# Differential attention: map 1's exponentials in PSUM, the scale in the queries, low query halves on 128 rows, shorter column steps

## Chip, cores and metric

The kernel runs on one core of one Trainium2 chip. The metric is device time in microseconds (us) of one execution, the median over several runs; lower is better. A profiled execution gives, beside its time, a trace with every engine's instructions: TensorE (PE, with its weight loads as PEld), VectorE (DVE), ScalarE (ACT), GpSimd (POOL) and SyncE's DMA queue (SPq).

## Reference

A two-layer diffusion backbone: 512 latent tokens, 256 context tokens, width 1024, one batch, fp32. Layer 0 mixes tokens with DeltaNet and retention heads, layer 1 with differential attention, and each layer ends in a convolutional feed-forward block. The change lies nearly all in layer 1's attention, 8 heads, each with two softmax maps of head size 64 over 768 keys and values of 128 columns:

```
def diff_mix(q, k, v, lam):
    """q (2,B,H,Lq,d), k (2,B,H,Lk,d), v (B,H,Lk,dv): (softmax(q1 k1) - lam softmax(q2 k2)) v."""
    s = jnp.einsum('cbhqd,cbhkd->cbhqk', q, k).astype(jnp.float32) * DIFF_HD ** -0.5
    p = jax.nn.softmax(s, -1)
    a = p[0] - lam * p[1]
    return jnp.einsum('bhqk,bhkd->bhqd', a.astype(v.dtype), v)
...
    def finish(o):
        o = rms_norm(o) * subln_w.astype(f32) * (1.0 - lambda_init)
        return (merge_heads(o).astype(w_out.dtype) @ w_out).astype(h.dtype)
```

Before it, `project` forms q, k and v from the layer's input and turns q and k by rotary angles. Only the 512 latent tokens are queries here.

## The kernel before

A scheduler places every instruction: the program is a sequence of tile operations with priorities, and each engine then has a fixed order that follows from them. Instructions wait on semaphores for their operands and for buffers to come free.

The attention is done head pair by head pair, four pairs. While `attend` works on pair p, the projections of pair p+1 (`project`) fill TensorE between its steps; during the last pair the filler is the output projection (`sums`). A matrix product of fp32 quality is made of three products of rounded halves ("hi" and "lo", names whi, wlo, hTh, hTl): every projection tile is a chain of `opj` matmuls of 128x256, three for each block of the inner dimension. DVE and POOL make the low halves of the weights (line 148), ACT the high ones (line 147).

`project` ends, for queries, with a rotation (`rope`: DVE lines 1575 and 1579, POOL line 1581), four transposes into a PSUM tile `oT_ps`, and `q_evac`, which takes that tile apart into SBUF tiles `oq`. The low 64 partitions (LO) hold map 0, the high 64 (HI) map 1. Tile q[0] holds map 0's rounded queries, in both halves of the partitions; q[1] does so for map 1; q[2] has the remainders, map 0 in LO and map 1 in HI. Keys (`ok`, `k_evac`) carry the rounded value in one half of the partitions and the remainder in the other, so one matmul over 128 rows gives q_hi*(k_hi + k_lo). `oT_ps` and `opj` share two PSUM buffers ("wo").

A step of `attend` is one of a head's four query tiles: 8 steps in a pair, 32 in all. A step does

- scores: for each map, two matmuls over 128 rows (512 and 256 columns) into a PSUM tile `sc` (two buffers for all), then two over the 64 rows of q[2],
- for each map: a row maximum `mx` on DVE (line 1665), its scaling on DVE (1666), the exponential on ACT (1668) into the SBUF tile `pt`, row sums into `Zs` (in the trace oZ),
- the factor `nl` on DVE (1672, 1673), one column, and the combination pt0 + nl*pt1 on DVE (1676), 768 columns,
- six transposes of pt into `aT_ps`, copies to `aT` by ACT (four blocks) and DVE (two, line 1684), six matmuls with the values into the same `aT_ps`, a copy to `oall` on DVE (1688) and a square on ACT (1689) for the norm.

After a head's four steps the norm is closed by a chain of 128x4 operations on DVE: lines 1693 to 1695, an rsqrt by iteration (lines 127 to 136, names rs_h, rs_y, rs_w), line 1697, and four products of 128x128 (1699).

Of the kernel before, what the change touches and what calls it, by code (L numbers as in the profile page):

```python
# [20 lines left out]
P = 128  # L21
# [76 lines left out]
class Net:  # L98
# [177 lines left out]
    def setup(self):  # L276
# [22 lines left out]
        self.cpad = cp.tile([P, KT, 32], F32, name="cpad")  # L299
        nc.gpsimd.memset(self.cpad, 0.0)  # L300
# [218 lines left out]
    def even_mixer(self, accst):  # L519
        w_in = self.a["e_w_in"][0]  # L520
        with ExitStack() as outer:
            with ExitStack() as right:
                p2 = self.pool(right, "d2", bufs=2, side="right")
                self.p2b = lambda: self.pool(right, "d2b", bufs=2, side="right")
# [1015 lines left out]
    def odd_mixer(self, acc_st):  # L1540
        nc, a = self.nc, self.a
        v, g, s_ = nc.vector, nc.gpsimd, nc.scalar
        with ExitStack() as st0:
            y = self.hT
            pj = self.pool(st0, "ps_opj", bufs=2, space=PSUM)
            with ExitStack() as st:
# [13 lines left out]
                lp = cpl.tile([P, 4, DH], F32, name="lp")  # L1560
                nc.scalar.dma_start(out=lp, in_=a["o_lambda"][0].partition_broadcast(P))
                l2 = cpl.tile([P, 2], F32, name="l2")
                for i in range(2):
                    v.tensor_mul(lp[:, 2 * i], lp[:, 2 * i], lp[:, 2 * i + 1])
                    v.reduce_sum(l2[:, i:i + 1], lp[:, 2 * i], axis=AX.X)
                s_.activation(l2, l2, AF.Exp)
                nlam = cpl.tile([P, 1], F32, name="nlam")
                v.tensor_sub(nlam, l2[:, 1:2], l2[:, 0:1])
                v.tensor_scalar_add(nlam, nlam, -LAMBDA_INIT)

                def rope(ps, t, out):

                    pv, ov = (x.rearrange("p (t h f n) -> p t h f n", t=2, h=4, f=2) for x in (ps, out))
                    b = p2.tile([P, 2, 4, 2, 32], F32, tag="ob", name="ob")
# [26 lines left out]
                def project(pr, passes, hd):  # L1601
# [3 lines left out]
                    hd["q"] = [hp.tile([P, 2, LAT], F32R, tag=f"oq{j}", name="oq") for j in range(3)]  # L1605
# [40 lines left out]
                def attend(h, q, k, vt, i):  # L1646
# [4 lines left out]
                    for t in range(NLT):  # L1651
                        pr = []
                        scs = [scp.tile([P, 1024], F32, tag="sc", name="sc") for c in range(2)]
                        for c in range(2):
                            for k0, n in ((0, 512), (512, 256)):
                                self.mm(scs[c][:, k0:k0 + n], q[c][:, i, t * P:(t + 1) * P], k[c][:, i, k0:k0 + n],
                                        stop=False)

                        for k0, n in ((0, 512), (512, 256)):
                            for c, rows in enumerate((LO, HI)):  # L1660
                                self.mm(scs[c][:, k0:k0 + n], q[2][rows, i, t * P:(t + 1) * P], k[c][rows, i, k0:k0 + n],
                                        start=False)
                        for c, sc in enumerate(scs):
                            mx = pb.tile([P, 1], F32, tag="mx", name="mx")
# [5 lines left out]
                            pr.append(pt)  # L1670
# [144 lines left out]
```

## Time and profile before

| | us |
|---|---|
| median of three runs (lowest, highest) | 2107.94 (2104.75, 2113.5) |
| the profiled execution | 2102.7 |
| its span in the trace | 2100.9 |
| PE busy | 1961.3 (93%) |
| DVE, POOL, ACT busy | 1272.7, 777.8, 703.8 |

The trace's time axis begins with the span. The attention of layer 1 lies between 1326 and 1665 us: the first three pairs up to 1592, the last pair behind it. The projections of its first pair lie ahead of it, from about 1255. PE's rows give a start and a duration; a matmul's end is modelled and overlaps the next one's start, so what one costs is read from start to start. A bracket behind a row gives the idle time ahead of it on its engine and what released it.

### The profile page before, as it was taken

To read this page: it belongs to the slowest core of one execution; us is meant where nothing else is said; L and a number is where in the kernel's file an instruction comes from. 1 tells how busy PE (TensorE), PEld (TensorE's weight loads), DVE (VectorE), ACT (ScalarE), POOL (GpSimd) and SP (SyncE) were. 2 spreads that over 40 slices of the span, in tenths; PEclk is the share of its full clock that TensorE was granted. 3 is DMA by queue.
4 is the path that set the end of the run, shared out by engine and by line. 5 is a ranking of instruction groups with operands and counts; after the bars stand their busy time and mean duration, and the time that the engine had idled before them with its cause. 6 is when DMAs were issued, how large, how long until landed. Compare 5 with 4: busy or idle time off the path is not lost. (4 is left out here: it accounts for less than half of the span.)

```text
span 2100.9 us, 33593 instructions
## 1 busy us (share of the span) xinstructions
PE 1961.3 (93%) x13766; PEld 1668.8 (79%) x13766; DVE 1272.7 (61%) x2534; ACT 703.8 (33%) x1228; POOL 777.8 (37%) x412
## 2 busy tenths in 40 slices
PE   6989999999898999999999998999897989999997
PEld 4777677878898988888888877878786887888886
DVE  2354755544358676565656574567667688756567
ACT  3331343423244422222222243444444443323231
POOL 1233223212322344444444433212123036666572
PEclk8999999999999999999999999999997999999999
DMA  8546344455523321111111112011102223232221
GB/s 264 161 129 177 110 133 139 146 172 173 171 81 121 115 76 61 61 61 61 61 61 61 61 61 68 21 41 41 41 31 71 80 101 121 94 106 96 85 81 40
DMA packets 195586, 201.34 MB, mean 96 GB/s; under 512 B 21112, under 2 KB 183512, under 8 KB 195432
## 3 DMA queue, kind: packets, MB, share of 16 engines
q1 hardware_dynamic: 194136, 197.57, 29.9%
q8 instruction: 108, 1.77, 0.4%
q10 hardware_dynamic: 1296, 1.62, 0.3%
q14 instruction: 46, 0.38, 0.1%
HBM read 185.89 MB, written 13.27 MB: 95 GB/s over the span
## 5 line engine op out<-in xcount | busy, mean ns | idle before, releaser
L148 POOL TENSOR_TENSOR wlo<-raw,whi 128x2048 fp32r<-128x2048 f32 (+2 forms) x154 | 413.2, 2709 | 490.1 <-ACT whi L147 457.1
L1442 DVE SCALAR_TENSOR_TENSOR ac<-g_ps,fconvT,ac 128x441 f32<-128x441 f32 (+2 forms) x352 | 243.6, 694 | 190.7 <-ACT ac L1431 181.0
L147 ACT CAST whi<-raw 128x2048 fp32r<-128x2048 f32 (+2 forms) x177 | 200.4, 1169 | 373.7 <-PE d_ps L115 162.2
L115 PE MATMUL d_ps<-whi,hh 128*128 128x512 f32 x440 | 176.1, 400 | 11.5 <-DVE gt L1391 6.6
L115 PE MATMUL d_ps<-wlo,hh 128*128 128x512 f32 x440 | 172.9, 393 | 0.0
L115 PE MATMUL d_ps<-whi,hl 128*128 128x512 f32 x440 | 172.3, 392 | 0.6 <-DVE hl L148 0.6
L115 PE MATMUL opj<-whi,hTh 128*128 128x256 f32 x512 | 151.3, 295 | 1.1 <-ACT oq L1592 1.1
L115 PE MATMUL g_ps<-hTl,whi 128*128 128x512 f32 (+1 forms) x384 | 145.1, 378 | 2.9 <-POOL hTl L148 2.9
L115 PE MATMUL opj<-whi,hTl 128*128 128x256 f32 x512 | 147.4, 288 | 0.0
L115 PE MATMUL opj<-wlo,hTh 128*128 128x256 f32 x512 | 147.2, 288 | 0.0
L115 PE MATMUL u_ps<-hTh,whi 128*128 128x512 f32 (+1 forms) x384 | 144.7, 377 | 0.0
L115 PE MATMUL u_ps<-hTh,wlo 128*128 128x512 f32 (+1 forms) x384 | 144.6, 377 | 0.0
L115 PE MATMUL u_ps<-hTl,whi 128*128 128x512 f32 (+1 forms) x384 | 144.6, 376 | 0.0
L115 PE MATMUL g_ps<-hTh,whi 128*128 128x512 f32 (+1 forms) x384 | 144.5, 376 | 0.0
L115 PE MATMUL g_ps<-hTh,wlo 128*128 128x512 f32 (+1 forms) x384 | 144.2, 376 | 0.0
L115 PE MATMUL fpj<-whi,hTh 128*128 128x256 f32 x432 | 127.0, 294 | 5.6 <-DVE kT L550 4.7
L115 PE MATMUL fpj<-wlo,hTh 128*128 128x256 f32 x432 | 127.0, 294 | 0.0
L115 PE MATMUL fpj<-whi,hTl 128*128 128x256 f32 x432 | 126.0, 292 | 0.0
L115 PEld LDWEIGHTS d_ps<-whi,hh 128*128 128x128 f32 x440 | 82.9, 188 | 38.9 <-DVE gt L1391 17.0
L115 PEld LDWEIGHTS opj<-whi,hTh 128*128 128x128 f32 x512 | 98.4, 192 | 7.2 <-issue 4.5
L115 PEld LDWEIGHTS opj<-whi,hTl 128*128 128x128 f32 x512 | 98.3, 192 | 2.8 <-issue 2.4
L115 PEld LDWEIGHTS opj<-wlo,hTh 128*128 128x128 f32 x512 | 98.5, 192 | 2.3 <-issue 1.2
(465 smaller groups left out, 5023.0 us busy)
## 6 DMA issues: line engine op xcount, KB each, us to landing
mraw<-in_mod_w_dram SPq DMA_DIRECT2D x80, 512.0 KB
raw<-in_f_w_gate_dram SPq DMA_DIRECT2D x22, 1024.0 KB
raw<-in_f_w_up_dram SPq DMA_DIRECT2D x22, 1024.0 KB
raw<-in_f_w_down_dram SPq DMA_DIRECT2D x22, 1024.0 KB
raw<-in_o_w_qkv_dram SPq DMA_DIRECT2D x12, 1024.0 KB
raw<-in_e_w_in_dram SPq DMA_DIRECT2D x10, 1024.0 KB
mraw<-in_mod_w_dram SPq DMA_DIRECT2D x32, 256.0 KB
raw<-in_e_w_in_dram SPq DMA_DIRECT2D x12, 512.0 KB
```

Of the source, the lines that this page charges most:

```text
L115: self.nc.tensor.matmul(out, lhsT=lhsT, rhs=rhs, start=start, stop=stop)
L147: self.nc.scalar.copy(h, r)
L148: lo_eng.tensor_sub(l, r, h.bitcast(F32))
L1442: v.scalar_tensor_tensor(out=o, in0=pv[:, r0 + di:r1 + di, c0 + dj:c1 + dj], scalar=cw[(di + 1) * 3 + dj + 1], in1=o, op0=ALU.mult, op1=AL ...
```

## The change

1. Scores. There are four query tiles: q[0] and q[1] as before, and q[2], q[3] hold the remainders of map 0 and map 1, each in both halves of the partitions. A step's low matmuls go over 128 rows, two for each map, and stand directly behind that map's high ones.
2. The factor 64^-0.5 is multiplied into the queries in `q_evac`. An evacuation has six ACT operations where it had four, and its two DVE operations become scalar_tensor_tensor. The maximum comes out negated from the reduction; the 64 scalings of mx are gone, and so is the scale of the exponential.
3. Map 1's exponential is written over its own scores in PSUM; the combination reads it there. The `sc` buffer of map 1 is read for the last time by the combination (before: by the exponential).
4. `nl` is made by a tensor_scalar with two column operands in place of a scalar_tensor_tensor.
5. The end of a head loses a reciprocal and three 128x4 products on DVE, and gains a 128x4 square on ACT and a 128x4 addition on DVE.
6. Buffers: `cpad`, a constant, moves into a pool of layer 0's mixer; the small tiles for lambda are in a pool of their own that is closed at once; `ob` has one buffer in place of two.

```
 def q_evac(q, ps, cs):
-    s_.copy(q[0][LO, :, cs], ps[LO])
-    s_.copy(q[1][HI, :, cs], ps[HI])
-    v.tensor_sub(q[2][LO, :, cs], ps[LO], q[0][LO, :, cs].bitcast(F32))
-    v.tensor_sub(q[2][HI, :, cs], ps[HI], q[1][HI, :, cs].bitcast(F32))
-    s_.copy(q[0][HI, :, cs], ps[LO])
-    s_.copy(q[1][LO, :, cs], ps[HI])
+    for c, src in enumerate((ps[LO], ps[HI])):
+        own, other = (LO, HI) if c == 0 else (HI, LO)
+        s_.activation(q[c][own, :, cs], src, AF.Copy, scale=DH ** -0.5)
+        v.scalar_tensor_tensor(out=q[2 + c][own, :, cs], in0=src, scalar=DH ** -0.5,
+                               in1=q[c][own, :, cs].bitcast(F32), op0=ALU.mult, op1=ALU.subtract)
+        s_.activation(q[c][other, :, cs], src, AF.Copy, scale=DH ** -0.5)
+        s_.copy(q[2 + c][other, :, cs], q[2 + c][own, :, cs].bitcast(F32))
...
 for c in range(2):
-    for k0, n in ((0, 512), (512, 256)):
-        self.mm(scs[c][:, k0:k0 + n], q[c][:, i, t * P:(t + 1) * P], k[c][:, i, k0:k0 + n],
-                stop=False)
-for k0, n in ((0, 512), (512, 256)):
-    for c, rows in enumerate((LO, HI)):
-        self.mm(scs[c][:, k0:k0 + n], q[2][rows, i, t * P:(t + 1) * P], k[c][rows, i, k0:k0 + n],
-                start=False)
+    for j in (0, 2):
+        for k0, n in ((0, 512), (512, 256)):
+            self.mm(scs[c][:, k0:k0 + n], q[j + c][:, i, t * P:(t + 1) * P],
+                    k[c][:, i, k0:k0 + n], start=(j == 0), stop=(j == 2))
 for c, sc in enumerate(scs):
     mx = pb.tile([P, 1], F32, tag="mx", name="mx")
-    v.reduce_max(mx, sc[:, :TOK], axis=AX.X)
-    v.tensor_scalar_mul(mx, mx, -(DH ** -0.5))
-    pt = pb.tile([P, TOK], F32, tag=f"p{c}", bufs=2 - c, name="pt")
-    s_.activation(pt, sc[:, :TOK], AF.Exp, scale=DH ** -0.5, bias=mx[:, 0:1],
-                  accum_out=Zs[:, t, c:c + 1])
+    v.reduce_max(mx, sc[:, :TOK], axis=AX.X, negate=True)
+    p = pb.tile([P, TOK], F32, tag="p0", name="pt") if c == 0 else sc[:, :TOK]
+    s_.activation(p, sc[:, :TOK], AF.Exp, bias=mx[:, 0:1], accum_out=Zs[:, t, c:c + 1])
...
-v.scalar_tensor_tensor(out=nl, in0=nl, scalar=Zs[:, t, 0:1], in1=nlam,
-                       op0=ALU.mult, op1=ALU.mult)
-v.scalar_tensor_tensor(out=pr[0], in0=pr[1], scalar=nl[:, 0:1], in1=pr[0],
+v.tensor_scalar(out=nl, in0=nl, scalar1=Zs[:, t, 0:1], scalar2=nlam[:, 0:1],
+                op0=ALU.mult, op1=ALU.mult)
+v.scalar_tensor_tensor(out=pt, in0=scs[1][:, :TOK], scalar=nl[:, 0:1], in1=pt,
                        op0=ALU.mult, op1=ALU.add)
...
-rz = pb.tile([P, NLT], F32, tag="orz", name="orz")
-v.reciprocal(rz, Zs[:, :, 0])
-v.tensor_mul(ss, ss, rz)
-v.tensor_mul(ss, ss, rz)
-r = self.rsqrt(pb, ss, NLT, 1.0 / (2 * DH), NORM_EPS, "on")
-v.tensor_mul(r, r, rz)
+zz = pb.tile([P, NLT], F32, tag="orz", name="orz")
+s_.activation(zz, Zs[:, :, 0], AF.Square, scale=math.sqrt(2 * DH * NORM_EPS))
+v.tensor_add(ss, ss, zz)
+r = self.rsqrt(pb, ss, NLT, 1.0 / (2 * DH), 0.0, "on")
```

The instructions' order on three engines, each at one place. First PE in a step of the first pair that alternates with projections, row by row (in the trace 1403.4 to 1407.8 us). Rows give line, operation, tiles and output; `sc` of 128x512 and 128x256 are score matmuls. The first row of before is the step's last high piece, the four `sc` rows behind it are its low ones:

```order
6955 L115 MATMUL sc<-ok,oq 128x256
6956 L115 MATMUL opj<-whi,hTh 128x256
6957 L115 MATMUL sc<-ok,oq 128x512
6958 L115 MATMUL opj<-wlo,hTh 128x256
6959 L119 MATMUL aT_ps<-ident,pt 128x128 x6
6960 L115 MATMUL sc<-ok,oq 128x512
6961 L115 MATMUL opj<-whi,hTl 128x256
6962 L115 MATMUL sc<-ok,oq 128x256
6963 L115 MATMUL opj<-whi,hTh 128x256
6964 L115 MATMUL sc<-ok,oq 128x256
6965 L115 MATMUL aT_ps<-ov,aT 128x128 x6
```

And after, from that step's second map on:

```order
6964 L115 MATMUL sc<-ok,oq 128x512
6965 L115 MATMUL opj<-whi,hTh 128x256
6966 L115 MATMUL sc<-ok,oq 128x256
6967 L115 MATMUL aT_ps<-ov,aT 128x128 x6
6968 L115 MATMUL opj<-wlo,hTh 128x256
6969 L115 MATMUL sc<-ok,oq 128x512
6970 L115 MATMUL opj<-whi,hTl 128x256
6971 L115 MATMUL sc<-ok,oq 128x256
6972 L115 MATMUL opj<-whi,hTh 128x256
```

Score and projection matmuls still alternate; the low matmuls moved from the end of the step into each map's own group of four.

Second, ACT at the first evacuation of queries that falls into the first pair's steps (at 1372.8 us in the trace; they are the second pair's queries); the numbers behind names tell tiles apart (`oT_ps_13311` and `oT_ps_13312` are the same tile of before and after). Before:

```order
612 L1587 CAST oq_12939<-oT_ps_13311 64x2x256
613 L1588 CAST oq_12940<-oT_ps_13311 64x2x256
614 L1591 CAST oq_12939<-oT_ps_13311 64x2x256
615 L1592 CAST oq_12940<-oT_ps_13311 64x2x256
616 L147 CAST whi_13835<-raw_13833 128x2048
617 L1668 ACTIVATE pt_13500,oZ_13486<-sc_13487,mx_13497 128x768
618 L1668 ACTIVATE pt_13505,oZ_13486<-sc_13488,mx_13502 128x768
```

And after:

```order
618 L1591 ACTIVATE oq_12945<-oT_ps_13312 64x2x256
619 L1594 ACTIVATE oq_12945<-oT_ps_13312 64x2x256
620 L1595 CAST oq_12947<-oq_12947 64x2x256
621 L1591 ACTIVATE oq_12946<-oT_ps_13312 64x2x256
622 L1666 ACTIVATE pt_13499,oZ_13486<-sc_13487,mx_13497 128x768
623 L1666 ACTIVATE sc_13488,oZ_13486<-sc_13488,mx_13501 128x768
624 L1594 ACTIVATE oq_12946<-oT_ps_13312 64x2x256
625 L1595 CAST oq_12948<-oq_12948 64x2x256
626 L147 CAST whi_13819<-raw_13817 128x2048
```

The last read of `oT_ps`, row 615 before and row 624 now, moved behind both exponentials of a step.

Third, DVE at the end of the first pair's second head, with the combination of the step that runs beside it (L1676 before, L1674 now). Before:

```order
1445 L1672 RECIPROCAL nl<-oZ 128x1
1446 L134 TENSOR_TENSOR rs_w<-rs_y 128x4
1447 L1673 SCALAR_TENSOR_TENSOR nl<-nl,oZ,nlam 128x1
1448 L135 TENSOR_TENSOR rs_w<-rs_w,rs_h 128x4
1449 L1688 COPY oall<-aT_ps 128x128
1450 L136 SCALAR_TENSOR_TENSOR rs_y<-rs_w,rs_y 128x4
1451 L1676 SCALAR_TENSOR_TENSOR pt<-pt,nl 128x768
1452 L1697 TENSOR_TENSOR rs_y<-rs_y,orz 128x4
1453 L1699 SCALAR_TENSOR_TENSOR oall<-oall,rs_y,sub 128x128 x4
```

And after:

```order
1432 L135 TENSOR_TENSOR rs_w<-rs_w,rs_h 128x4
1433 L1670 RECIPROCAL nl<-oZ 128x1
1434 L1686 COPY oall<-aT_ps 128x128
1435 L136 SCALAR_TENSOR_TENSOR rs_y<-rs_w,rs_y 128x4
1436 L1671 TENSOR_SCALAR nl<-nl,oZ,nlam 128x1
1437 L1696 SCALAR_TENSOR_TENSOR oall<-oall,rs_y,sub 128x128 x4
1438 L1674 SCALAR_TENSOR_TENSOR pt<-sc,nl,pt 128x768
```

The combination moved from ahead of the four products of the head's end to behind them.

## Rows read from the trace of the kernel before

**Rows 1.** The page, section 1: busy us, share of the span, instructions.

```profile
PE 1961.3 (93%) x13766; PEld 1668.8 (79%) x13766; DVE 1272.7 (61%) x2534; ACT 703.8 (33%) x1228; POOL 777.8 (37%) x412
```

**Rows 2.** Windows: length, busy PE PEld DVE ACT POOL (instructions), PEclk, DMA share, GB/s.

```profile
1326.00:1592.00 266.00, 245.61 (x1797) 217.63 (x1796) 169.66 (x371) 113.20 (x224) 54.75 (x21) 0.99 0.11 37
1592.00:1665.00 73.00, 61.76 (x372) 50.08 (x371) 58.53 (x127) 34.99 (x75) 19.71 (x5) 0.84 0.20 66
```

**Rows 3.** PE's waits, first three pairs: us in total, times, longest us.

```profile
PE aT_ps L119 <- DVE pt L1676: 14.3, 10, 3.0
PE oT_ps L119 <- POOL otok L1581: 4.6, 6, 2.4
PE opj L115 <- ACT oq L1592: 1.1, 3, 0.6
```

**Rows 4.** PE's waits, 1255 to 1326 us, where layer 1's projections start.

```profile
PE ln_ps L119 <- ACT acc L1240: 4.1, 2, 2.8
```

**Rows 5.** Timeline of PE: a step whose maps go together (start, us, line, operation).

```profile
1372.49 1.49 PE L115 MATMUL sc<-ok,oq 128*128 128x512 f32 x8
1373.91 0.39 PE L115 MATMUL opj<-whi,hTh 128*128 128x256 f32 x1
```

**Rows 6.** Timeline of PE: one map of a step that goes map by map.

```profile
1326.32 1.05 PE L115 MATMUL sc<-ok,oq 128*128 128x512 f32 x4
1327.30 0.39 PE L115 MATMUL opj<-whi,hTh 128*128 128x256 f32 x1
```

**Rows 7.** Timeline of PE: a step that alternates with projection matmuls.

```profile
1403.43 0.40 PE L115 MATMUL sc<-ok,oq 128*128 128x512 f32 x1
1403.67 0.28 PE L115 MATMUL opj<-whi,hTh 128*128 128x256 f32 x1
1403.79 0.28 PE L115 MATMUL sc<-ok,oq 128*128 128x256 f32 x1
...
1405.36 0.81 PE L119 MATMUL aT_ps<-ident,pt 128*128 128x128 f32 x6
1406.10 0.50 PE L115 MATMUL sc<-ok,oq 64*128 64x512 f32 x1
...
1407.79 0.38 PE L115 MATMUL aT_ps<-ov,aT 128*128 128x128 f32 x1
```

**Rows 8.** Timeline of all engines around one factor nl.

```profile
1380.76 4.54 POOL L148 TENSOR_TENSOR wlo<-raw,whi 128x2048 fp32r<-128x2048 f32 x1
...
1381.15 4.17 DVE L1673 SCALAR_TENSOR_TENSOR nl<-nl,oZ,nlam 128x1 f32<-128x1 f32 x1
```

**Rows 9.** Tile nl, whole span: duration ns min/median/max, first and last start.

```profile
L1673 DVE SCALAR_TENSOR_TENSOR nl<-nl,oZ,nlam x32: 208/219/4168, 1334.6 to 1659.4; 128x1 f32<-128x1 f32 x32
L1676 DVE SCALAR_TENSOR_TENSOR pt<-pt,nl x32: 1006/1018/1020, 1334.8 to 1659.6; 128x768 f32<-128x768 f32 x32
```

**Rows 10.** Tile mx, whole span.

```profile
L1666 DVE TENSOR_SCALAR mx<-mx x64: 127/144/156, 1329.8 to 1657.3; 128x1 f32<-128x1 f32 x64
L1668 ACT ACTIVATE pt<-sc,mx x64: 881/902/914, 1330.0 to 1657.5; 128x768 f32<-128x768 f32 x64
```

**Rows 11.** Timeline of DVE in the last pair.

```profile
1610.62 0.14 DVE L1666 TENSOR_SCALAR mx<-mx 128x1 f32<-128x1 f32 x1
...
1611.55 3.63 DVE L1697 TENSOR_TENSOR rs_y<-rs_y,orz 128x4 f32<-128x4 f32 x1
```

**Rows 12.** Timeline of POOL in the same stretch.

```profile
1605.76 9.40 POOL L185 TENSOR_TENSOR raw<-raw,gate 128x2048 f32<-128x2048 f32 x2 [12.48 <-DMA raw<-in_o_w_out_dram]
```

**Rows 13.** Timeline of ACT and DVE: one evacuation of a query tile.

```profile
1373.56 1.14 DVE L1699 SCALAR_TENSOR_TENSOR oall<-oall,rs_y,sub 128x128 f32<-128x128 f32 x4
...
1374.62 0.68 DVE L1589 TENSOR_TENSOR oq<-oT_ps,oq 64x512 fp32r<-64x512 f32 x1
...
1376.03 0.58 ACT L1591 CAST oq<-oT_ps 64x512 fp32r<-64x512 f32 x1 [2.09 <-DVE oq L1590]
```

**Rows 14.** Tile ac (feed-forward): a DVE operation with one PSUM and one SBUF input.

```profile
L1442 DVE SCALAR_TENSOR_TENSOR ac<-g_ps,fconvT,ac x352: 662/678/745, 700.8 to 2067.1; 128x441 f32<-128x441 f32 x88, 128x504 f32<-128x504 f32 x44, 128x448 f32<-128x448 f32 x44
```

More of the change, by code (lines that the diff above doesn't have):

```diff
@@ L298, in setup @@
         nc.vector.memset(self.lneps, LN_EPS)
-        self.cpad = cp.tile([P, KT, 32], F32, name="cpad")
-        nc.gpsimd.memset(self.cpad, 0.0)
         self.hs = {}
@@ L523, in even_mixer @@
                 p2 = self.pool(right, "d2", bufs=2, side="right")
+                self.cpad = p2.tile([P, KT, 32], F32, bufs=1, name="cpad")
+                self.nc.gpsimd.memset(self.cpad, 0.0)
                 self.p2b = lambda: self.pool(right, "d2b", bufs=2, side="right")
@@ L1559, in odd_mixer @@
                 v.tensor_scalar_mul(sub, sub, 1.0 - LAMBDA_INIT)
[L1560 to L1566, printed above, removed]
-                nlam = cpl.tile([P, 1], F32, name="nlam")
-                v.tensor_sub(nlam, l2[:, 1:2], l2[:, 0:1])
-                v.tensor_scalar_add(nlam, nlam, -LAMBDA_INIT)
+                nlam = cpl.tile([P, 1], F32, name="nlam")
+                with ExitStack() as tmp:
+                    lpp = self.pool(tmp, "olp")
+                    lp = lpp.tile([P, 4, DH], F32, name="lp")
+                    nc.scalar.dma_start(out=lp, in_=a["o_lambda"][0].partition_broadcast(P))
+                    l2 = lpp.tile([P, 2], F32, name="l2")
+                    for i in range(2):
+                        v.tensor_mul(lp[:, 2 * i], lp[:, 2 * i], lp[:, 2 * i + 1])
+                        v.reduce_sum(l2[:, i:i + 1], lp[:, 2 * i], axis=AX.X)
+                    s_.activation(l2, l2, AF.Exp)
+                    v.tensor_sub(nlam, l2[:, 1:2], l2[:, 0:1])
+                    v.tensor_scalar_add(nlam, nlam, -LAMBDA_INIT)
                 def rope(ps, t, out):
                     pv, ov = (x.rearrange("p (t h f n) -> p t h f n", t=2, h=4, f=2) for x in (ps, out))
-                    b = p2.tile([P, 2, 4, 2, 32], F32, tag="ob", name="ob")
+                    b = p2.tile([P, 2, 4, 2, 32], F32, tag="ob", bufs=1, name="ob")
                     v.tensor_mul(out.rearrange("p (t x n) -> p t x n", t=2, n=32),
@@ L1604, in project @@
                     hp = odd if pr % 2 else even
-                    hd["q"] = [hp.tile([P, 2, LAT], F32R, tag=f"oq{j}", name="oq") for j in range(3)]
+                    hd["q"] = [hp.tile([P, 2, LAT], F32R, tag=f"oq{j}", name="oq") for j in range(4)]
                     hd["k"] = [hp.tile([P, 2, TOK], F32R, tag=f"ok{j}", name="ok") for j in range(2)]
@@ L1670, in attend @@
-                            pr.append(pt)
+                            v.reduce_max(mx, sc[:, :TOK], axis=AX.X, negate=True)
+                            p = pb.tile([P, TOK], F32, tag="p0", name="pt") if c == 0 else sc[:, :TOK]
+                            s_.activation(p, sc[:, :TOK], AF.Exp, bias=mx[:, 0:1], accum_out=Zs[:, t, c:c + 1])
+                            if c == 0:
+                                pt = p
                         nl = pb.tile([P, 1], F32, tag="nl", name="nl")
                         v.reciprocal(nl, Zs[:, t, 1:2])
-                        v.scalar_tensor_tensor(out=nl, in0=nl, scalar=Zs[:, t, 0:1], in1=nlam,
-                                               op0=ALU.mult, op1=ALU.mult)
@@ L1681, in attend @@
                             for j in range(n):
-                                self.tr(ps[:, j * P:(j + 1) * P], pr[0][:, (c0 + j) * P:(c0 + j + 1) * P])
+                                self.tr(ps[:, j * P:(j + 1) * P], pt[:, (c0 + j) * P:(c0 + j + 1) * P])
                             eng = s_.copy if n == 4 else v.tensor_copy
@@ L1688, in attend @@
                         v.tensor_copy(oall[:, t, hc], o)
-                        s_.activation(pr[0][:, :P], oall[:, t, hc], AF.Square, accum_out=ss[:, t:t + 1])
+                        s_.activation(pt[:, :P], oall[:, t, hc], AF.Square, accum_out=ss[:, t:t + 1])
                         if t < NLT - 1:
                             yield
-                    rz = pb.tile([P, NLT], F32, tag="orz", name="orz")
-                    v.reciprocal(rz, Zs[:, :, 0])
-                    v.tensor_mul(ss, ss, rz)
-                    v.tensor_mul(ss, ss, rz)
-                    r = self.rsqrt(pb, ss, NLT, 1.0 / (2 * DH), NORM_EPS, "on")
-                    v.tensor_mul(r, r, rz)
+                    zz = pb.tile([P, NLT], F32, tag="orz", name="orz")
+                    s_.activation(zz, Zs[:, :, 0], AF.Square, scale=math.sqrt(2 * DH * NORM_EPS))
+                    v.tensor_add(ss, ss, zz)
+                    r = self.rsqrt(pb, ss, NLT, 1.0 / (2 * DH), 0.0, "on")
                     for t in range(NLT):
```

1 line of the change is left out of this document (removed).

## The prediction, made before the changed kernel ran

> **What bounds the kernel now.** I read the page's busy shares first: PE is busy 93% of the span [rows 1], so time is gained where PE does less or waits less. Then the windows over layer 1's attention, the only long stretch that the change touches [rows 2]. In the first three pairs PE is busy 245.6 of 266 us: PE sets the pace, and its 20.4 us of idle time are waits. In the last pair, 73 us, PE has 11.2 us without work, the granted clock is 0.84 of full speed, and DVE is busy 58.5: there the chain of DVE and ACT operations of each step counts, and PE's matmuls do not. PE's waits in the first three pairs [rows 3] are in the main for the combination, 14.3 us in ten waits, then 4.6 us for POOL's part of the rotation, which the change leaves alone.
>
> Why the combination is late is seen on all engines' timeline [rows 8]: a POOL operation of 4.54 us starts, the factor nl, one column, begins 0.39 us later on DVE and takes 4.17 us, up to the end of POOL's. Undisturbed it takes 0.22 us (the median over 32), the longest 4.17 [rows 9].
>
> **Scores on 128 rows.** Read from start to start, a full-row matmul of 512 columns takes 0.24 us and one of 256 takes 0.12 [rows 7]. After the change a step has four of each: 1.44 us. Before, a step's cost depends on its neighbours. Where both maps go together, the eight matmuls counted by the row and their low pairs take 1373.91 - 1372.49 = 1.42 us [rows 5]: nothing to gain. Where maps go one at a time, a map takes 1327.30 - 1326.32 = 0.98 us, 1.96 a step [rows 6]: 0.52 to gain. Where the pieces alternate with projections, the step spans 1407.79 - 1403.43 = 4.36 us, of which seven projection matmuls of 0.12 (0.84) and six transposes (1406.10 - 1405.36 = 0.74) are not its own; 2.78 remain [rows 7]: 1.34 to gain. By the order on PE each of the three pairs has four steps of the first kind; the first pair has two each of the others (3.7 us), the next two have three of the dearest and one of the middle kind (4.5 us each). Sum 12.7 us; I take **-13**. Bounds: all twelve at 0.52, 6; all at 1.34, 16. The last pair is not paced by PE: nothing.
>
> The Trainium skill speaks against this edit (TensorEngine Tiling (Array Packing), Key Properties): different tiles can execute in parallel, so two 64-row matmuls could cost one, and a change of mode drains the array. By the first half alone the paired steps would lose 0.36 us each by going to 128 rows, 4 us over the twelve of the first three pairs. The row of the paired step shows no such parallel gain (1.42 us, the same as full rows); its second half agrees with what the alternating step pays.
>
> **nl as a tensor_scalar, map 1 in PSUM.** Is a 128x1 tensor_scalar still held up by POOL? The 64 scalings of mx are that form, with one column operand fewer, and none took over 0.156 us [rows 10]. One of them, at 1610.62, took 0.14 while POOL worked and a two-input operation begun 0.93 us later took 3.63 [rows 11, 12]. So I take 0.2 us always. The combination then has one PSUM and one SBUF input; of that form 352 operations of 441 to 504 columns took 0.66 to 0.75 us and never more [rows 14], some 1.0 to 1.1 for 768 columns by proportion, as now (1.02, [rows 9]). The stall goes. The exponential written to PSUM: no row has ACT writing there; I take the 0.90 us of now [rows 10]. Below it a gain of at most the same 0.9 is conceivable, above it twice the time; in the first three pairs either is hidden, since ACT is busy 113 of 266 us, in the last pair twice the time would cost up to 8 x 0.9 = 7 us.
>
> The Trainium skill would have it otherwise (SBUF — State Buffer, Who interferes with whom): tensor_scalar can enter a two-port mode and then contends with GpSimd, whoever comes first blocking the other. By it the new nl would be held as the old one was; the rows of the one-column scalings are against that, so I give it a small chance, as the fourth rival.
>
> **What is late next.** With the stall gone, PE waits for other things. (a) The first evacuation of queries in each pair. Now ACT's last two reads begin at 1376.03 and end at 1377.2 [rows 13]; PE's next projection tile needs that PSUM buffer and waits 0.6 us at most [rows 3]. In the order after, the fourth read of oT_ps stands behind the third copy and two exponentials: DVE's part still starts at 1374.62 (a head's four products are ahead of it), then 0.68, three ACT operations of 0.58, two exponentials of 0.9 and 0.58: 1374.62 + 0.68 + 1.74 + 1.8 + 0.58 = 1379.4, so 2.2 us later. (b) The second evacuation has the same form, with an exponential fewer in front of PE's need: 1.3 us, where the longest wait for a combination (3.0) was. (c) At the end of a pair the combination now stands behind the head's rsqrt chain and its four products on DVE. The products take 1.14 us [rows 13], the chain's share is not to be had from one row; with transposes and copies that come late in turn I take 3.5 us, between 1.1 and twice the longest wait of now, 6. (d) 0.5 for what is left. In all 7.5 us a pair, 22.5 for three, against 20.4 now: **+2**. Bounds: if these waits fall into PE's remaining projection work, only the 4.6 + 1.1 us of the rotation and the old q wait stay, -15; if each is half as long again, +13.
>
> **Removed work on DVE**: 64 scalings at 0.144 (9.2 us) and four small operations a head. In the first three pairs DVE is busy 170 of 266 us, so it is hidden behind PE. 16 more ACT copies of 0.58 us (9.3) are hidden too, but for the place in (a), (b).
>
> **Last pair.** Each of eight steps has a chain shorter by two scalings and their hand-overs (0.3 us), and the first exponential starts a maximum earlier, but three POOL operations still hold the rsqrt chain, whose column products have two SBUF inputs [rows 11, 12]: 8 x 0.3 = 2.4, less what is waited for anyway. I take **-2**, bounds -6 (one stall as in [rows 8] gone as well) and +5 (a step later by the new place of the combination).
>
> **Start of layer 1 and layer 0.** PE's transposes of the new input come 12 projection matmuls later in the order, 12 x 0.12 = 1.4 us, and PE waits 4.1 us there for ACT [rows 4]: **-1.5**, bounds -4 and +1. The move of cpad makes a few constant loads of layer 0 wait for a buffer; I take 0, ±2. One buffer for `ob` I cost at nothing: its next use waits for POOL's addition, and where POOL was late it shows already in the 4.6 us of [rows 3].
>
> **Sum** against the profiled execution: -13 + 2 - 2 - 1.5 = -14.5, 2102.7 to 2088.2. The median of the runs shown is 5.2 us above that execution: 2107.94 - 14.5 = 2093.4, so I forecast **2093 us**.
>
> **Rivals.**
> 1. The stalls vanish and nothing follows: waits -15 in place of +2, 2093 - 17 = 2076. For it: the evacuation's additional time lies beside projections that PE may still have to do. Against: PE's order puts the next projection tile close behind, and two PSUM buffers are all it has.
> 2. The evacuation eats the gain: each of six in-pair evacuations delays PE by 2.9 (2.2 as in (a) and a further copy of 0.58 with its hand-over), the head's end as in (c): 6 x 2.9 against 3 x 3.5, +7 on the forecast, 2100. It would be within 0.5%.
> 3. Slower: map 1's score buffer is held until the combination has read it, so the next step's scores start later by reciprocal, nl, combination and hand-overs, 0.16 + 0.22 + 1.02, about 1.4 us. In the last pair and the twelve alternating and single steps that is (8 + 12) x 1.4 = 28, 2121; it decides from 0.8 us a step over all 32. For it: two sc buffers in all, and steps of the last pair 73/8 = 9 us apart at most. Against: in the first three pairs a step comes each 266/24 = 11 us, DVE is busy for 7.1 of them and ACT for 4.7, and when the buffer is late, projections are there to do.
> 4. The edit of nl does not do what it says: POOL still holds it. Then a stall of 3.0 a pair stays beside (a) to (c) and covers (b) only: 3 x (3.0 - 1.3) = 5, 2098.
>
> **Chances.** Forecast (2085 to 2097) 0.45; rival 1 0.18; rival 2 0.20; rival 3 0.08; rival 4 0.09. A measurement here tells about 0.5%, 10.5 us: faster is below 2097.4, slower above 2118.5. Faster: nearly all of the forecast, rival 1 and a little of 2 and 4, 0.65; slower: rival 3 without its weaker forms, 0.07; same 0.28. The range leaves out rival 3 and the far half of rival 1: 2076 to 2105; the likeliest case's own is 2085 to 2097.
>
> **What would show it.** In the profile after: no nl above 0.25 us; no 64-row matmul, and an alternating step at 1.4 us net; a wait of PE's `opj` for ACT's oq of 1 to 3 us twice a pair; the combination behind the head's products. The forecast is wrong if PE's waits in the three pairs sum to under 10 us or above 30, if PE waits for `sc` buffers in the first three pairs, or if the exponential into PSUM takes other than 0.9 us.

## The result, and the profile after

The changed kernel is faster: 2080.05 us median (2075.46 to 2082.24, four runs) against 2110.72 for the kernel before in the same job; ratio 0.9848, 95% interval 0.9824 to 0.9871. That is 31 us less, where 14.5 were forecast: the sign and the range held, the forecast gain was half of the measured one.

The page's first section, the windows over the first three pairs and over the last pair (length, busy PE, PEld, DVE, ACT, POOL, granted clock, DMA share, GB/s), and PE's waits in the first three pairs:

```profile
PE 1944.0 (94%) x13766; PEld 1671.6 (80%) x13766; DVE 1246.6 (60%) x2446; ACT 716.3 (34%) x1252; POOL 776.1 (37%) x412
```

```profile
1331.80:1571.00 239.20, 229.93 (x1798) 215.88 (x1797) 148.71 (x311) 124.02 (x248) 52.69 (x21) 1.00 0.12 41
...
1571.00:1640.00 69.00, 52.46 (x366) 47.49 (x365) 52.08 (x105) 34.65 (x73) 19.74 (x5) 0.90 0.21 69
```

```profile
PE sc L115 <- ACT pt L1666: 3.0, 3, 1.1
PE opj L115 <- ACT oq L1594: 1.6, 3, 0.5
PE oT_ps L119 <- POOL otok L1583: 1.5, 6, 0.5
PE aT_ps L119 <- DVE pt L1674: 1.2, 2, 0.6
```

And two of PE's waits in the last pair:

```profile
PE wo_ps L115 <- DVE hTl L1706: 8.9, 1, 8.9
...
PE sc L115 <- DVE pt L1674: 1.3, 1, 1.3
```

The first window answers to [rows 2] of before: 266 us have become 239.2. PE's busy time fell by 15.7 us (245.6 to 229.9), its idle time by 11.1 (20.4 to 9.3). The wait for the combination, 14.3 us before [rows 3], is 1.2. The evacuation costs 4.6: 1.6 where a projection waits for `oT_ps`, and the 3.0 for `sc`. The row names ACT's `pt`, which is map 0's exponential: PE waits for map 0's buffer, and that exponential stands on ACT behind four operations of the evacuation (shown under "What is late next"). Map 1's buffer, which the change holds until the combination (DVE L1674) has read it, costs PE nothing in the first three pairs and 1.3 us in the last.

To set the two traces side by side I use the starts of four matmuls: layer 1's first projection, its first score, its last projection, and the first `u_ps` of its feed-forward block. Us between them:

| stretch | before | after | difference | forecast |
|---|---|---|---|---|
| to the first projection (layer 0) | 1262.2 | 1272.0 | +9.8 | 0 |
| to the first score | 64.1 | 59.9 | -4.2 | -1.5 |
| first three pairs | 268.7 | 241.7 | -27.0 | -11 |
| last pair and output projection | 119.4 | 116.1 | -3.3 | -2 |

The 9.8 us of layer 0 are not the change's. In the changed kernel's profiled execution PE ran at a lower granted clock in places there; a kernel with the same order of layer 0 did not, and kernels with the old order began layer 1 as late (1272.6 us in experiment 5, 1274.9 in experiment 6). The profiled execution of before was an early one: 2102.7 us against a median of 2110.72.

### The profile page after: what moved, and what is told of

Its sections match the earlier page's. It is cut to its first block, busy times and chain, and to the rows that moved or that the text cites. A ratio compares the mean times of both kernels' runs of the same rounds, so it can differ in the third digit from the quotient of the medians.

```text
span 2076.8 us, 33472 instructions
## 1 busy us (share of the span) xinstructions
PE 1944.0 (94%) x13766; PEld 1671.6 (80%) x13766; DVE 1246.6 (60%) x2446; ACT 716.3 (34%) x1252; POOL 776.1 (37%) x412
## 5 line engine op out<-in xcount | busy, mean ns | idle before, releaser
L115 PE MATMUL opj<-whi,hTh 128*128 128x256 f32 x512 | 146.6, 286 | 2.1 <-ACT oq L1594 1.6
L115 PE MATMUL c_ps<-hTh,wlo 128*128 128x256 f32 x352 | 98.9, 281 | 0.0
L115 PE MATMUL c_ps<-hTh,whi 128*128 128x256 f32 x352 | 98.8, 281 | 0.0
```

Of the source, the lines that this page charges most:

```text
L115: self.nc.tensor.matmul(out, lhsT=lhsT, rhs=rhs, start=start, stop=stop)
```

## Experiments

Times are medians of several runs, with the ratio to the kernel before, run in the same job (its medians: 2113.84 for experiments 1 to 4, 2113.92 for 5 to 8, 2110.77 for 9 to 11). The ratio is estimated from the runs and is not the quotient of the two medians: the two differ by up to 0.3%, inside the interval. Stretches are between the same four matmuls as above.

**1. Only nl back.** The changed kernel, with

```
-v.tensor_scalar(out=nl, in0=nl, scalar1=Zs[:, t, 0:1], scalar2=nlam[:, 0:1],
-                op0=ALU.mult, op1=ALU.mult)
+v.scalar_tensor_tensor(out=nl, in0=nl, scalar=Zs[:, t, 0:1], in1=nlam,
+                       op0=ALU.mult, op1=ALU.mult)
```

> The changed kernel with nl made by the old scalar_tensor_tensor (two SBUF columns as inputs) instead of the tensor_scalar; all else as changed. Theory A (the tensor_scalar is what freed DVE from POOL's operations): nl stalls of 1 to 4 us come back, PE waits for the combination about 14 us in the first three pairs, and the time rises by 10 to 15 us over the changed kernel, to 2090 to 2095. Theory B (the stalls went because the order and the moment of nl changed): no nl above 0.3 us, time within 3 us of the changed kernel, 2080.

Measured: 2096.22, ratio 0.9915 (0.9886 to 0.9943), 16 us above the changed kernel (14 by the ratios), 1 us beyond the expected range. Theory A. Tile nl, PE's largest wait and the window of the first three pairs:

```profile
L1671 DVE SCALAR_TENSOR_TENSOR nl<-nl,oZ,nlam x32: 203/219/3019, 1337.9 to 1651.1; 128x1 f32<-128x1 f32 x32
```

```profile
PE aT_ps L119 <- DVE pt L1674: 13.1, 5, 2.7
```

```profile
1330.30:1587.50 257.20, 236.59 (x1795) 222.93 (x1795) 159.37 (x311) 124.52 (x248) 52.26 (x21) 0.97 0.12 38
```

The stalls are back, and with them 18 us: 11.3 more of PE's idle time and 6.7 more of busy time, at a granted clock of 0.97 instead of 1.00. The matmuls are the same, and 3% of 236.6 us is 7.1 (an estimate), so the lower clock accounts for the additional busy time. In the changed kernel itself the new form never took more than 0.274 us:

```profile
L1671 DVE TENSOR_SCALAR nl<-nl,oZ,nlam x32: 254/273/274, 1339.4 to 1632.7; 128x1 f32<-128x1 f32 x32
L1674 DVE SCALAR_TENSOR_TENSOR pt<-sc,nl,pt x32: 1006/1018/1019, 1339.8 to 1633.0; 128x768 f32<-128x768 f32 x32
```

**2. Only the 64 rows back.** The changed kernel, with one tile q[2] and

```
+for k0, n in ((0, 512), (512, 256)):
+    for c, rows in enumerate((LO, HI)):
+        self.mm(scs[c][:, k0:k0 + n], q[2][rows, i, t * P:(t + 1) * P], k[c][rows, i, k0:k0 + n],
+                start=False)
```

behind the high matmuls of both maps.

> The changed kernel with the low query halves back on 64 rows (one tile q[2], four low matmuls over 64 rows behind the high ones, four scaled ACT copies and two DVE operations in an evacuation); the scale in the queries, PSUM exponential and nl as changed. Theory A (full rows are worth PE time): PE busy in the first three pairs rises by 13 to 16 us and the time by as much, 2093 to 2096. Theory B (PE time of the scores is hidden, the gain is all waits): under 4 us, 2080 to 2084.

Measured: 2108.36, ratio 0.9976 (0.9958 to 0.9993): 28 us above the changed kernel, far more than expected. Window, and PE's largest wait there, in the first three pairs:

```profile
1331.70:1589.80 258.10, 245.85 (x1804) 218.39 (x1803) 157.80 (x312) 116.86 (x236) 54.29 (x21) 0.98 0.12 38
```

```profile
PE aT_ps L119 <- DVE pt L1680: 8.4, 3, 4.0
```

PE's busy time rose by 15.9 us, as Theory A had it. The rest are stalls in new places: neither nl nor the combination is held, but a product in a head's rsqrt chain (line 135) is, ahead of a combination (by form, DVE: count, total and mean ns; had all been undisturbed, the 15 would have taken 0.16 us each):

```profile
L135 DVE TENSOR_TENSOR rs_w<-rs_w,rs_h 128x4 f32<-128x4 f32 x15 | 13.9, 929 | 0.5
```

In all the first three pairs took 260.7 us instead of 241.7. And the last pair with the output projection took 125.2 us instead of 116.1. So the order that each edit brings decides which DVE operation meets POOL's.

**3. cpad back in the constants**, in the changed kernel:

```
-self.cpad = p2.tile([P, KT, 32], F32, bufs=1, name="cpad")
+self.cpad = cp.tile([P, KT, 32], F32, name="cpad")
```

> The changed kernel with cpad back in the pool of constants; with it the instruction order of layer 0 is that of before again. In the changed kernel's trace layer 0 ends some 10 us later than before, in three stretches at a lower granted clock. Theory A (the move of cpad costs layer 0 these 10 us): layer 1's projections start at 1262 instead of 1272 us, time about 2070. Theory B (the lower clock in layer 0 comes and goes from execution to execution or with the layout): time within 3 us of 2080, and the low stretches are there in some executions of either.

Measured: 2074.03, ratio 0.982 (0.979 to 0.9849); the interval overlaps that of the changed kernel. Layer 1 began at 1267.5 us. Neither theory's numbers came (1262 and 2070, or 2077 to 2083).

**4. Only the buffer moves**, in the kernel before: cpad, the lambda tiles and `ob` as in part 6 of the change.

> The kernel before with only the three moves of buffers (cpad into the pool of layer 0's mixer, the lambda tiles in a pool of their own, one buffer for ob); no arithmetic changes. Theory A (the move of cpad costs layer 0 10 us): 2120 against 2110, layer 1's projections start 10 us later than in the kernel before. Theory B: within 3 us of the kernel before.

Measured: 2110.95, ratio 0.9991 (0.9972 to 1.001): nothing. Layer 1 began at 1268.8. The same 40 us of layer 0 in the changed kernel and in this one, which have the same order there:

```profile
430.00:470.00 40.00, 36.13 (x567) 28.99 (x566) 12.38 (x43) 11.96 (x34) 7.35 (x7) 0.87 0.48 142
```

```profile
430.00:470.00 40.00, 38.29 (x616) 31.47 (x615) 15.69 (x57) 13.20 (x38) 8.32 (x8) 1.00 0.56 167
```

The granted clock was 0.87 in one and 1.00 in the other. With the old order of layer 0 layer 1 began at 1267.5 in experiment 3 and at 1272.6 in experiment 5; experiment 8, with the new order, began it at 1275.3: the spread of layer 0 does not follow the move, Theory B.

**5. Only nl**, in the kernel before (the lines of experiment 1 the other way round).

> The kernel before with nl alone as the tensor_scalar of the changed kernel; the combination still reads two SBUF tiles. Theory A (POOL holds whichever DVE operation with two SBUF inputs comes next): nl takes 0.27 us always, the combination behind it takes up to 4 us where nl did, PE's waits for it stay at about 14 us in the first three pairs, time 2106 to 2114, no gain. Theory B (the short one-column operation was the one that suffers): no combination above 1.1 us, PE's waits fall by 10 us and more, time 2092 to 2098.

Measured: 2107.19, ratio 0.9979 (0.9962 to 0.9995). Theory A: the stall moved by one instruction, with PE's wait at 11.2 us instead of 14.3 and the first three pairs at 265.1 us instead of 268.7. Tile nl (whole span) and PE's wait in these pairs:

```profile
L1673 DVE TENSOR_SCALAR nl<-nl,oZ,nlam x32: 261/273/275, 1345.0 to 1666.7; 128x1 f32<-128x1 f32 x32
L1676 DVE SCALAR_TENSOR_TENSOR pt<-pt,nl x32: 1004/1019/4664, 1345.3 to 1667.0; 128x768 f32<-128x768 f32 x32
```

```profile
PE aT_ps L119 <- DVE pt L1676: 11.2, 7, 2.8
```

The combination, which in the kernel before never took more than 1.020 us [rows 9], now takes up to 4.66.

**6. PSUM and nl**, in the kernel before:

```
-pt = pb.tile([P, TOK], F32, tag=f"p{c}", bufs=2 - c, name="pt")
+pt = pb.tile([P, TOK], F32, tag="p0", name="pt") if c == 0 else sc[:, :TOK]
```

and nl as in experiment 5.

> The kernel before with map 1's exponential written over its scores in PSUM and nl as the tensor_scalar, nothing else (scalings of mx, 64-row low halves, old evacuation and head end stay). Theory A (these two edits together free the combination from POOL): no nl and no combination is held, PE's waits for the combination in the first three pairs fall from 14 to under 5 us, time 2092 to 2098. The rival by which the held score buffer costs a step about 1.4 us: PE waits for sc in the first three pairs by 10 us and more, time 2110 or above.

Measured: 2105.68, ratio 0.9967 (0.9948 to 0.9986): less than expected. The first three pairs behave as Theory A says, 250.9 us instead of 268.7; their window and all of PE's waits over half a microsecond:

```profile
1339.30:1587.60 248.30, 240.99 (x1797) 215.50 (x1796) 152.53 (x371) 115.67 (x228) 53.77 (x20) 0.99 0.13 41
```

```profile
PE oT_ps L119 <- POOL otok L1581: 5.0, 6, 2.4
PE opj L115 <- ACT oq L1592: 1.4, 3, 0.6
PE aT_ps L115 <- DVE aT L1684: 0.7, 3, 0.2
```

No wait for the combination is left, and none for a score buffer, so the slower rival is refuted for this stretch. But 9 of the 18 us were given back in the last pair and the output projection (128.5 us instead of 119.4), where PE now waits for the low half of the head's transposed output, itself behind DVE's head end:

```profile
PE wo_ps L115 <- DVE hTl L1709: 6.6, 3, 5.3
PE aT_ps L119 <- DVE pt L1676: 4.7, 2, 2.4
```

**7. Only the rows**, in the kernel before, with the buffer moves that make room:

```
-hd["q"] = [hp.tile([P, 2, LAT], F32R, tag=f"oq{j}", name="oq") for j in range(3)]
+hd["q"] = [hp.tile([P, 2, LAT], F32R, tag=f"oq{j}", name="oq") for j in range(4)]
...
+s_.copy(q[2][HI, :, cs], q[2][LO, :, cs].bitcast(F32))
+s_.copy(q[3][LO, :, cs], q[3][HI, :, cs].bitcast(F32))
```

and the score loop of the change.

> The kernel before with the low query halves on 128 rows (four query tiles, two more ACT copies an evacuation behind the reads of the PSUM tile) and the moves of buffers that make room; scale, exponentials, nl and head end as before. Theory A (PE time of the scores counts in full): PE busy in the first three pairs falls from 245.7 to about 231, the nl stalls stay, time 2096 to 2099. Theory B (what PE saves it then waits for, since the stalls of the combination are set by DVE and POOL): PE busy falls, its waits rise by as much, time 2106 to 2112.

Measured: 2104.25, ratio 0.9967 (0.9948 to 0.9986). Theory B in its mechanism, 2 us below its range: the first three pairs took 267.7 us against 268.7.

```profile
1330.50:1595.60 265.10, 237.43 (x1797) 225.31 (x1796) 173.57 (x373) 122.75 (x240) 51.81 (x21) 0.95 0.11 37
```

```profile
PE aT_ps L119 <- DVE pt L1676: 17.3, 13, 3.1
PE aT_ps L115 <- DVE mx L1666: 6.9, 2, 3.5
```

PE is busy 8.3 us less, at a granted clock of 0.95 instead of 0.99, and waits 7.3 us more. Four hundredths of 237 us are some 9 us (an estimate): part of what the rows save is spent on the lower clock. The 0.33% come from ahead of and behind the pairs (60.0 and 117.1 us).

**8. Evacuation with the reads first**, in the changed kernel:

```
 s_.activation(q[0][LO, :, cs], ps[LO], AF.Copy, scale=sc_)
 s_.activation(q[1][HI, :, cs], ps[HI], AF.Copy, scale=sc_)
...
 s_.activation(q[0][HI, :, cs], ps[LO], AF.Copy, scale=sc_)
 s_.activation(q[1][LO, :, cs], ps[HI], AF.Copy, scale=sc_)
 s_.copy(q[2][HI, :, cs], q[2][LO, :, cs].bitcast(F32))
 s_.copy(q[3][LO, :, cs], q[3][HI, :, cs].bitcast(F32))
```

> The changed kernel with the evacuation of queries in another order: both own copies, both DVE operations, both other copies, and the two copies that read SBUF last, so that the PSUM tile is read for the last time two ACT operations earlier. If the longer evacuation costs PE the 3 to 4 us a pair that the prediction took, 2070 to 2074; if PE has other work in that time, as its trace of the changed kernel has it (waits of 0.5 us, three times), within 3 us of the changed kernel.

Measured: 2079.21, ratio 0.9848 (0.9824 to 0.9872), as the changed kernel. PE's waits of the same kinds in the first three pairs:

```profile
PE opj L115 <- ACT oq L1597: 2.7, 3, 1.0
...
PE sc L115 <- ACT pt L1670: 0.2, 1, 0.2
```

The wait for `oT_ps` is longer than before the edit (2.7 against 1.6), but the one for map 0's score buffer is gone (0.2 against 3.0), and the first three pairs took 238.6 us instead of 241.7. So the order of the evacuation is worth about 3 us in this stretch. The whole time does not show them: layer 1 began 3.3 us later in this trace (1275.3), and the two intervals nearly coincide. The scheduler also put one of the two copies that read SBUF ahead of the last two reads of the PSUM tile, so the edit did not place all reads first.

**9. Rows, PSUM and nl together**, in the kernel before: experiments 6 and 7 in one.

> The kernel before with the low halves on 128 rows, map 1's exponential in PSUM, nl as the tensor_scalar and the buffer moves together; the scalings of mx, the unscaled queries, the scaled exponentials and the old head end stay. The rows alone gave 0.33%, PSUM with nl alone 0.33%. Theory A (the two edits need each other: what PE saves on rows only counts when POOL no longer holds the combination): first three pairs at 240 to 246 us against 268.7, time 2080 to 2088. Theory B (the edits only add, and the rest of the change, scale and head end, brings the other 15 us): first three pairs near 250, time 2094 to 2100.

Measured: 2085.82, ratio 0.9853 (0.9819 to 0.9887). Theory A: the first three pairs take 239.2 us.

```profile
1334.80:1571.40 236.60, 228.33 (x1798) 215.61 (x1797) 155.00 (x373) 122.85 (x240) 52.34 (x21) 1.00 0.13 41
```

Apart, the two gave 1.0 and 17.8 us in that stretch; together 29.5. The scale in the queries, the missing scalings and the shorter head end show no gain there: the changed kernel takes 241.7, and its waits for map 0's score buffer (3.0 us, here 0.2) cover the difference. Behind it the changed kernel is shorter, 116.1 us for the last pair and the output projection against 124.1; which of those edits does that was not tried.

**10. POOL's operations in pieces**, in the kernel before:

```
-lo_eng.tensor_sub(l, r, h.bitcast(F32))
+m = n // self.lparts
+for j in range(self.lparts):
+    e = slice(j * m, (j + 1) * m)
+    lo_eng.tensor_sub(l[:, e], r[:, e], h[:, e].bitcast(F32))
```

with lparts 4 for layer 1's q, k and v weights.

> The kernel before with POOL's low halves of layer 1's weights in four operations of 512 columns instead of one of 2048; no DVE instruction changes. Theory A (a DVE operation with two SBUF inputs is held to the end of the POOL operation that runs when it comes, and may go between two): no nl in the first three pairs above 1.3 us where they went to 4.2, PE's waits for the combination fall from 14 to 3 to 7 us, time 2 to 12 us below the kernel before. Theory B (it is held until POOL has nothing left to do): nl up to 4 us as before, no gain.

Measured: 2099.97, ratio 0.9942 (0.992 to 0.9964), 11 us less than before with the same DVE order. The first three pairs took 258.9 us; PE's wait for the combination there:

```profile
PE aT_ps L119 <- DVE pt L1682: 8.8, 11, 1.5
```

The longest wait is half of the 3.0 of before. Theory A, with a correction: nl and then the combination are each held by a piece (nl up to 0.95 us in these pairs, the combination up to 2.02), so the sum fell less (8.8, not 3 to 7).

**11. Pieces in the changed kernel**, with cpad in the constants, the last pair's products of weights and gate in pieces too.

> The changed kernel with cpad back in the pool of constants and with POOL's operations of layer 1 in pieces: low halves of the weights in four of 512 columns, the last pair's products with the gate in four of 512 each. If pieces let the head's chain and products on DVE pass between them (held 4.4 and 4.5 us in the last pair of the changed kernel), the last pair and the output projection behind it take 110 to 114 us instead of 116, and the time is 2064 to 2072. If not, or if DVE is held by each piece in turn, within 3 us of the run with cpad back, 2074.

Measured: 2072.2, ratio 0.9798 (0.9764 to 0.9833), like experiment 3; the last stretch 115.9 us. The expectation's second half came true. DVE's end of a head in the last pair, in the changed kernel and here:

```profile
1584.50 4.35 DVE L136 SCALAR_TENSOR_TENSOR rs_y<-rs_w,rs_y 128x4 f32<-128x4 f32 x1
1588.89 4.80 DVE L1696 SCALAR_TENSOR_TENSOR oall<-oall,rs_y,sub 128x128 f32<-128x128 f32 x2
```

```profile
1584.34 0.38 DVE L136 SCALAR_TENSOR_TENSOR rs_y<-rs_w,rs_y 128x4 f32<-128x4 f32 x1
1584.75 5.14 DVE L1703 SCALAR_TENSOR_TENSOR oall<-oall,rs_y,sub 128x128 f32<-128x128 f32 x4
```

Here each of the four products is held by one piece (1.32 to 1.36 us each). A hold by short operations is short, but there are as many as there are operations that suffer it.

**12. The gate's products on DVE**, in the kernel of experiment 3:

```
-nc.gpsimd.tensor_mul(rv, rv, scale.unsqueeze(1).to_broadcast([P, KT, 256]))
+nc.vector.tensor_mul(rv, rv, scale.unsqueeze(1).to_broadcast([P, KT, 256]))
```

> The changed kernel with cpad back in the pool of constants and the last pair's two products of the output weights with the gate on DVE instead of POOL. On POOL they take 4.5 us each and hold DVE's head end for 4.4 and 4.5 us. If the hold is what the last pair waits for, DVE does both in about 2.2 us each, nothing of the head's end above 1.2 us is left, and the last pair with the output projection takes 110 to 114 us against 116: 2068 to 2072. If DVE's own busy time is the limit there (51 of 69 us before these 4.4 are added), 116 us and 2072 to 2078.

Measured: 2073.04, ratio 0.9793 (0.977 to 0.9816), in a job where before took 2115.47. The last stretch took 110.4 us instead of 116.0, as expected; the time was expected at 2068 to 2072. DVE there:

```profile
1582.85 2.29 DVE L185 TENSOR_TENSOR raw<-raw,gate 128x2048 f32<-128x2048 f32 x1
1585.05 1.14 DVE L1696 SCALAR_TENSOR_TENSOR oall<-oall,rs_y,sub 128x128 f32<-128x128 f32 x4
1586.10 2.29 DVE L185 TENSOR_TENSOR raw<-raw,gate 128x2048 f32<-128x2048 f32 x1
```

With POOL out of the way the four products take 1.14 us again. Its interval lies wholly below that of the changed kernel (0.9824 to 0.9871), but it overlaps those of experiments 3 and 11, whose medians are within 2 us. Against experiment 3, from which it differs by this edit alone, the 5.6 us of the last stretch are not shown in the whole time: in these two traces the start of layer 1 and the first three pairs took 3.3 us more.

## Why the prediction was right in sign and half in size

**nl and PSUM: right, and the core of the change.** Both are needed: nl alone hands the stall to the combination (experiment 5), nl undone alone brings it back (experiment 1). No nl above 0.276 us was measured in any kernel with the new form; so the fourth rival (still held) did not come. The sign named for it, no nl above 0.25 us, was set too low: undisturbed the new form takes 0.273. The third rival (map 1's score buffer, held until the combination has read it) did not come either: PE waits for that buffer 1.3 us in all, in the last pair, against the 0.8 us a step from which that rival would have decided.

**Scores: right in size, with one row misread.** -13 forecast, -15.7 of PE's busy time measured. Not all of it is the rows: in experiment 6, without them, PE was busy 4.7 us less than before, with 96 changes between 64- and 128-row matmuls in the first three pairs instead of 110. With the other edits in place the rows are worth 12.7 us of busy time (experiment 9 against 6) or 15.9 (experiment 2). The granted clock was 1.00 instead of 0.99, worth up to 2.5 of them (1% of 245.6).

The prediction read from the step's 1.42 us that paired 64-row matmuls do not run in parallel. They do. The low matmuls of the step in [rows 5], and a projection matmul with a single low one behind it, in the kernel before:

```profile
1373.37 0.50 PE L115 MATMUL sc<-ok,oq 64*128 64x512 f32 x2
1373.70 0.28 PE L115 MATMUL sc<-ok,oq 64*128 64x256 f32 x2
...
1404.50 0.28 PE L115 MATMUL opj<-whi,hTh 128*128 128x256 f32 x1
1404.71 0.49 PE L115 MATMUL sc<-ok,oq 64*128 64x512 f32 x1
```

Two take 0.50 us together, as one alone does [rows 7], and the four low matmuls take 0.54 us to the next projection (1373.91), where full rows take 0.72. The gain is lost at the changes of the row count: the projection ahead of a 64-row matmul starts 0.21 us before it, where 0.12 is usual. So both halves of what the prediction cites from the Trainium skill (TensorEngine Tiling (Array Packing), Key Properties: tiles work in parallel, a change of mode drains the array) agree with the trace, and in a paired step they nearly cancel. After the change such a step takes 1.47 us, 0.05 more:

```profile
1375.88 1.64 PE L115 MATMUL sc<-ok,oq 128*128 128x512 f32 x8
1377.35 0.28 PE L115 MATMUL opj<-whi,hTh 128*128 128x256 f32 x1
```

**What is late next: the step that failed.** The sum put 22.5 us of new waits in the place of the 20.4 that go; measured are 9.3. (a), (b): the evacuation is as long as worked out, here the first, 6.7 us from its first to its last read of the PSUM tile (6.6 by the prediction, from its first read in the kernel before, 1372.77, to 1379.4):

```profile
1376.16 0.59 ACT L1591 ACTIVATE oq<-oT_ps 64x512 fp32r<-64x512 f32 x1 [3.42 <-PE oT_ps L119]
...
1382.23 0.59 ACT L1594 ACTIVATE oq<-oT_ps 64x512 fp32r<-64x512 f32 x1
```

But PE comes late to the tile that it holds up, because it has a step's scores and projections to do first, and waits for half a microsecond. The evacuation's other price is map 0's exponential, which follows it on ACT; PE's next scores wait for that:

```profile
1380.33 0.90 ACT L1666 ACTIVATE pt<-sc,mx 128x768 f32<-128x768 f32 x1
1381.38 0.96 PE L115 MATMUL sc<-ok,oq 128*128 128x512 f32 x4 [1.06 <-ACT pt L1666]
...
1382.88 0.38 PE L115 MATMUL opj<-whi,hTh 128*128 128x256 f32 x1 [0.54 <-ACT oq L1594]
```

That is 1.6 us at the first evacuation of a pair and nothing at the second, 4.6 in three pairs where (a) and (b) had 10.5. I set the evacuation's length against PE's arrival of before, not against the order of work after. (c): the combination behind the head's end was counted at 3.5 us a pair; PE waited 1.2 us for combinations in all three pairs. The order named there was right; that the delay lay beside projections is what the short waits suggest, no run shows it by itself. (d) had 1.5 us for all else, though the prediction said that the change leaves the 4.6 of the rotation alone, so by its own premise the sum lacked 3. The rotation's wait was 1.5: that the sum had it right is luck. (With the rows and buffer moves alone, experiment 7, it is 1.6; in experiment 6 it stays at 5.0.) Rival 1 (stalls vanish and nothing follows, 5.7 us of waits, 2076) comes nearest in this stretch. Two of the prediction's own signs of being wrong came: waits under 10 us in the three pairs, and waits for `sc`, though for map 0's buffer and not as rival 3 has it.

**That terms may be added: not argued.** I added -13 for the rows to the rest without asking whether PE's savings reach the time. Alone, the rows gave 1.0 us in the pairs (experiment 7): what PE saves it waits for while DVE is held. With the stalls gone they are worth 11.7 us of the stretch (experiment 6 against 9, 250.9 to 239.2) or 19.0 (experiment 2), and the two together 29.5. The addition held because the same change removes the stalls; the prediction did not give that reason.

**Start and last pair.** -1.5 was -4.2: PE's wait for ACT at the transposes fell from 4.1 [rows 4] to 2.8, and that for the rotation from 2.6 to 0.8. -2 was -3.3, near. There two POOL operations (the prediction has three) still hold the head's end, 4.35 and 4.54 us, and PE waits 8.9 us for what follows it (`hTl`); with both on DVE the stretch is 5.6 us shorter (experiment 12).

**Baseline.** The prediction's rows come from an execution of 2102.7 us, lower than every timed run of the kernel before (2104.65 the lowest), and its forecast starts from a median of 2107.94. From the 2110.72 that the changed kernel was measured against, the same -14.5 would have given 2096, further from the measured 2080.

## What to carry to other kernels

When a stall comes from two engines that exclude each other, look at which operand lies where: moving one input of a per-step operation to PSUM, together with a new form of the small operation ahead of it, removed a stall that the small operation's change alone only handed on. Before adding the gain of less work on the busiest engine, ask whether what it waits for would move earlier too; if not, the gain turns into a wait. And price a longer operation by when its consumer arrives in the new order and by what stands behind it on its own engine, not by its own length.

## What the runs showed of the hardware

- A DVE operation with two SBUF inputs that starts while POOL works on a tensor_tensor waits to the end of that operation, however small it is itself: 0.22 us became 4.17 [rows 8, 9]. In the five kernels with the old nl, all 49 that began with over 0.3 us of a long POOL operation (over 0.9 us) to go were held. With POOL's work in pieces of 512 columns (1.3 us) it passes between two.
- The one-column tensor_scalar never waited (0.276 us at most over nine kernels); the combination with one PSUM input neither (1.021 at most). POOL was at work beside them: 74 of these nl and 91 of these combinations began as the 49 above did. The Trainium skill (SBUF — State Buffer, Who interferes with whom) has it that a DVE instruction with two SBUF inputs contends with a GpSimd one that reads SBUF, and one with at most one SBUF input, outside the two-port modes, does not; the trace agrees for the old nl and for both combinations. The section also has tensor_scalar among the operations that can contend, under conditions on its operands; in this case that is seen for wider forms (128x4 in experiment 11: 1.22 us where 0.16 is usual), not for one column.
- Two 64-row matmuls in different halves of the rows ran side by side (0.50 us for two as for one), and each change between 64 and 128 rows cost some 0.1 us (an estimate: 0.21 us from start to start ahead of a change, 0.12 without one).
- An exponential over its own input in PSUM took 0.875 us in the median, the one into SBUF 0.902:

```profile
L1666 ACT ACTIVATE pt<-sc,mx x32: 892/902/912, 1336.1 to 1627.7; 128x768 f32<-128x768 f32 x32
L1666 ACT ACTIVATE sc<-sc,mx x32: 863/875/895, 1337.6 to 1631.4; 128x768 f32<-128x768 f32 x32
```

- Layer 0 took 1262 to 1275 us to the first projection over the traces of these kernels, and the order of its instructions does not tell which; what makes the granted clock fall there in some executions stays open.
